# Moving every on-chip slot of a fused decoder layer to a 256-byte boundary

## The chip, the cores and the metric

The kernel runs on one core of a Trainium2 chip. The metric is the device time of one execution in microseconds (us); lower is better. SBUF is the on-chip memory; an address in it below is a byte address within one of its 128 partitions, the same in all of them. TensorE (PE) multiplies; VectorE (DVE), ScalarE (ACT) and GpSimd (POOL) do the rest; transfers are issued from SyncE's queue (SP).

## The reference

One layer on x of 1024 tokens by 1024 features, all in float32:

```
x = x + 0.5 * swiglu(rms_norm(x), w_gate, w_up, w_down)          # FF = 2816
h = rms_norm(x);  q,k,v,f | q,k,v | g_fox,g_sb = split(h @ w_in)
y_fox = softmax(q k^T/8 + cumulated log-forget-gates, causal) v   # 8 heads of 64
y_sb  = stick-breaking attention of the second q,k,v              # 8 heads of 64
x = x + (sigmoid(g_fox) * (y_fox @ w_branch_fox) + sigmoid(g_sb) * (y_sb @ w_branch_sb)) @ w_out
x = x + 0.5 * swiglu(rms_norm(x), ...)                            # second set of weights
x = x + sigmoid(rms_norm(x) @ w_ple_gate) * (p @ w_ple_proj)
```

## The kernel before

Every large product is done in the 32-bit reduced format (`float32r`) with each operand split into a high and a low part; three matmuls, high by high, high by low and low by high, stand for one. The split is an ACT copy and a subtraction (`split`, lines 103 and 104; `whigh` and `wlow`, lines 127 and 137). Most matmuls have a stationary operand of 128 by 128, which PE loads ahead of the matmul (an LDWEIGHTS, "PEld" in the profile), and a moving operand of 128 by 512 that is streamed through it. In the profile's `out<-a,b` of a matmul, a is the moving and b the stationary operand.

The work comes in this order, with the line of the matmul: the first FFN's gate and up products (lines 426 and 471, seven products in place of eight for each block of a two by two split), its down product (366), the projections of the attention stage (698, 706, 861), sixteen heads of attention (scores at 942 and 943, transposes at 994, values at 1016) woven with further projections, the branch products (706, 1223), the output product (366), the second FFN (426, 471, 366), and the gated embedding at the end (1490). Inside the two FFNs the order of all instructions is written out by hand; PE's own order is fixed by chained dependencies in the whole kernel. In an FFN the stationary operands of line 471 are split four products ahead (`prep`) into tiles whose tags rotate `("WL", "WL", "WL", "Q", "Q", "PT")`; the moving operands stay in tiles H, X and T.

All working tiles are slots of one pool, taken by tag in rotation:

```
BUFS = {"X": 2, "H": 4, "RAW": 2, "WH": 3, "WL": 3, "T": 4, "GF": 2, "RN": 2,
        "Q": 2, "KH": 2, "KL": 2, "Y": 2, "PT": 3}
```

A tag's slots are as large as its largest tile and stand one behind the other. X and H have 16,384 bytes a slot, the others 4096, except WH, WL and Y: these also hold a piece of `w_in` with 264 columns (256 of the values and 8 of the forget gates) as `[128, 4, 264]`, and so have 4224 bytes, 16.5 times 256. At address 0 stand 16,384 bytes of scratch for the descriptors of DMAs that software generates; the kernel issues none of these (its DMAs are all `nc.sync.dma_start` and one `nc.scalar.dma_start`). Behind them come four 32-byte constants, the kernel's own constants, small statistics, and from 19,328 (75.5 times 256) the slots.

That gives this remainder of the slots' start addresses divided by 256. All offsets within tiles at which the wide matmuls read are multiples of 256 bytes, so the remainder holds for the matmul's operand too. It is called the phase below.

| tag | before | after |
|---|---|---|
| X, PT, H, T, Q, GF, RN, RAW (all slots) | 128 | 0 |
| KH, KL (both slots) | 0 | 0 |
| WH | 128, 0, 128 | 0, 0, 0 |
| WL | 0, 128, 0 | 0, 0, 0 |
| Y | 128, 0 | 0, 0 |

The identity matrix for the transposes moves from phase 128 to 0 as well. Where the 264 columns are the moving operand, one row of them is 1056 bytes before (4 times 256 and 32) and 1088 after (4 times 256 and 64), so there the phase goes on by 32 or 64 from one block of 128 rows to the next.

Of the kernel before, what the change touches and what calls it, by code (L numbers as in the profile page):

```python
# [10 lines left out]
F32 = mybir.dt.float32  # L11
# [7 lines left out]
P = 128  # L19
# [11 lines left out]
BUFS = {"X": 2, "H": 4, "RAW": 2, "WH": 3, "WL": 3, "T": 4, "GF": 2, "RN": 2,  # L31
        "Q": 2, "KH": 2, "KL": 2, "Y": 2, "PT": 3}
# [4 lines left out]
def tile_hybrid_decoder_layer(  # L37
# [6 lines left out]
    nc = tc.nc  # L44
    cp = ctx.enter_context(tc.tile_pool(name="const", bufs=1))
    st = ctx.enter_context(tc.tile_pool(name="stats", bufs=4))
    sb = ctx.enter_context(tc.tile_pool(name="sb", bufs=2))
# [4 lines left out]
    def nm(s):  # L52
        uid[0] += 1
        return f"{s}_{uid[0]}"

    def slot(tag, shape, dt=F32):
        return sb.tile(shape, dt, tag=tag, bufs=BUFS[tag], name=nm(tag))

    def stat(shape, tag, bufs=4):
        return st.tile(shape, F32, tag=tag, bufs=bufs, name=nm(tag))  # L60
# [51 lines left out]
    def wraw_load(pieces, nk, n, tag="RAW"):  # L112
        raw = slot(tag, [P, nk, n])
        c = 0
        for src in pieces:
            w = src.shape[-1]
            nc.sync.dma_start(raw[:, :, c:c + w], src)
            c += w
        return raw
# [5 lines left out]
    def whigh(raw, nk, n, tag):  # L125
        hi = slot(tag, [P, nk, n], F32R)
        order("wh", nc.scalar.copy(hi[:], raw[:]))  # L127
        return hi

    def wlow(raw, hi, nk, n, tag, eng_lo=nc.gpsimd):  # L130
        lo = slot(tag, [P, nk, n], F32R)
        if nk == 1:
            parts = [(slice(None), slice(None), slice(i * n // 2, (i + 1) * n // 2)) for i in range(2)]
        else:
            parts = [(slice(None), slice(i * nk // 2, (i + 1) * nk // 2)) for i in range(2)]
        for part in parts:
            ins = eng_lo.tensor_sub(lo[part], raw[part], f(hi[part]))  # L137
            if eng_lo is nc.gpsimd:
                order("wl", ins)
        return lo  # L140

    def kp(w):
        return w.rearrange("(k p) n -> p k n", p=P)

    identf = cp.tile([P, P], F32, name="identf")
    make_identity(nc, identf[:])
    mask_fox = cp.tile([P, P], F32, name="mask_fox")
# [1399 lines left out]
```

## Time and profile before

| | |
|---|---|
| median of 3 runs | 2284.68 us (2284.53 to 2285.09) |
| span of the profiled execution | 2282.3 us |
| median less span (what lies around the span) | 2.4 us |
| PE busy in the span | 2260.2 us (99%) |
| DVE, ACT, POOL busy | 64%, 43%, 36% |
| granted TensorE clock | 1.00 in every stretch asked for |

The page gives the profiled execution's span and no time of its own beside it; the distance of 2.4 us between the runs' median and that span is carried over unchanged wherever a span is turned into a time. A matmul's duration in the profile contains its way through the array and overlaps the next matmul's; what a matmul costs in a row of them is the distance from its start to the next one's.

### The profile page before, as it was taken

Reading aid. Unit: us, or ns where it says so; the run is one execution under the profiler, and the core shown is the slowest. Engines: PE = TensorE matmul, PEld = TensorE weight load, DVE = VectorE, ACT = ScalarE, POOL = GpSimd, SP = SyncE. Lnnn points to the kernel's source line nnn. Section 1 sums busy time; section 2 is a strip of 40 time slices with the busy share of each in tenths; the row PEclk is TensorE's granted clock in tenths of the full one; section 3 lists DMA queues with packets and bytes.
Section 4 is the critical chain, followed back from the end, with each engine's and each line's share of the span. In section 5 each row is a group of like instructions: output and inputs, shape, how many; then the busy total and the mean of one; then the engine's idle time right before and its main releaser. Section 6 shows DMA issues by size and latency. Waiting matters only on the chain.

```text
span 2282.3 us, 30639 instructions
## 1 busy us (share of the span) xinstructions
PE 2260.2 (99%) x11462; PEld 1912.9 (84%) x11462; DVE 1459.6 (64%) x2199; ACT 977.7 (43%) x1741; POOL 828.1 (36%) x762
## 2 busy tenths in 40 slices
PE   8999999999999999999999999999999999999999
PEld 6888888888899999988988887888888888888887
DVE  8845555588863466666666675889655555778753
ACT  6333333333353555555555564245333333434431
POOL 2444444300033456554556654410544443200121
PEclk9999999999999999999999999999999999999999
DMA  4232323384333322132224245821423232656132
GB/s 139 102 116 84 125 83 125 137 315 158 115 120 118 99 86 74 48 89 70 52 56 116 61 150 173 298 109 59 139 84 125 83 125 79 259 193 218 63 102 84
DMA packets 187655, 275.49 MB, mean 121 GB/s; under 512 B 27113, under 2 KB 109417, under 8 KB 187506
## 3 DMA queue, kind: packets, MB, share of 16 engines
q1 hardware_dynamic: 187504, 273.53, 35.6%
q8 instruction: 90, 1.47, 0.3%
q14 instruction: 59, 0.48, 0.1%
q10 hardware_dynamic: 2, 0.00, 0.0%
HBM read 189.83 MB, written 75.27 MB: 116 GB/s over the span
## 4 chain that ended last, share of the span: by engine, by line
PE 94%; DVE 4%; ACT 1%; issue 1%; DMA 0%; DVEq 0%; ACTq 0%
PE ps L471 35%; PE ps L366 21%; PE ps L706 10%; PE ps L698 8%; PE ps L1490 4%; PE ps L1223 4%; PE ps L1016 3%; PE ps L994 2%; PE ps L426 1%; PE ps L943 1%; PE ps L942 1%; DVE RN L918 1%; PE ps L226 1%; PE ps L861 1%; DVE PT L997 0%
## 5 line engine op out<-in xcount | busy, mean ns | idle before, releaser
L366 PE MATMUL ps<-H,H 128*128 128x512 f32 x2184 | 497.8, 389 | 1.2 <-DVE X L374 1.2
L366 PEld LDWEIGHTS ps<-H,H 128*128 128x128 f32 x2184 | 409.4, 188 | 86.7 <-issue 2.0
L471 PE MATMUL ps<-H,WL 128*128 128x512 f32 x1008 | 244.3, 394 | 0.6 <-ACT WL L103 0.6
L471 PEld LDWEIGHTS ps<-H,WL 128*128 128x128 f32 x1008 | 189.7, 188 | 44.6 <-ACT WL L103 1.0
L706 PE MATMUL ps<-H,WH 128*128 128x512 f32 x768 | 210.5, 401 | 1.1 <-DVE PT L829 1.1
L706 PEld LDWEIGHTS ps<-H,WH 128*128 128x128 f32 x768 | 136.5, 188 | 24.4 <-DVE PT L829 1.6
L137 POOL TENSOR_TENSOR WL<-RAW,WH 128x512 fp32r<-128x512 f32 (+1 forms) x108 | 127.2, 1197 | 78.7 <-ACT WH L127 72.9
L137 POOL TENSOR_TENSOR WL<-Y,WH 128x512 fp32r<-128x512 f32 (+1 forms) x10 | 14.4, 1463 | 383.3 <-ACT WH L127 383.3
L997 DVE TENSOR_TENSOR PT<-ps,PT 128x512 fp32r<-128x512 f32 (+1 forms) x160 | 101.1, 633 | 76.0 <-ACT PT L996 74.9
L471 PE MATMUL ps<-H,Q 128*128 128x512 f32 x600 | 143.5, 390 | 0.0
L374 DVE SCALAR_TENSOR_TENSOR X<-ps,X 128x512 f32<-128x512 f32 x168 | 108.9, 685 | 50.9 <-PE ps L366 50.9
L698 PE MATMUL ps<-WH,H 128*128 128x256 f32 (+1 forms) x896 | 131.7, 286 | 1.9 <-DVE X L104 1.0
L471 PEld LDWEIGHTS ps<-H,Q 128*128 128x128 f32 x600 | 112.6, 188 | 23.9
L996 ACT CAST PT<-ps 128x512 fp32r<-128x512 f32 (+1 forms) x160 | 87.4, 548 | 95.6 <-PE ps L994 91.7
L471 PE MATMUL ps<-X,WL 128*128 128x512 f32 x504 | 123.5, 394 | 0.0
L698 PEld LDWEIGHTS ps<-WH,H 128*128 128x128 f32 x896 | 116.6, 189 | 3.7 <-DVE X L104 1.4
L471 PEld LDWEIGHTS ps<-X,WL 128*128 128x128 f32 x504 | 94.9, 188 | 21.8
L1016 PE MATMUL ps<-PT,X 128*128 128x256 f32 (+1 forms) x640 | 105.6, 283 | 5.9 <-DVE PT L997 5.8
L1016 PEld LDWEIGHTS ps<-PT,X 128*128 128x128 f32 x640 | 94.2, 189 | 18.6 <-DVE PT L997 9.3
L706 PE MATMUL ps<-H,WL 128*128 128x512 f32 x384 | 108.6, 399 | 0.0
L955 POOL TENSOR_TENSOR T<-T,l 128x128 f32<-128x128 f32 (+3 forms) x64 | 73.2, 1147 | 88.2 <-DVE l L954 85.8
L267 POOL TENSOR_TENSOR PT<-GF,RN 128x512 f32<-128x512 f32 x20 | 33.1, 1655 | 190.8 <-DVE GF L514 104.9
(400 smaller groups left out, 4737.2 us busy)
## 6 DMA issues: line engine op xcount, KB each, us to landing
hidden<-PT SPq DMA_DIRECT2D x40, 512.0 KB, 3.1
WH<-in_ffn_w_gate_dram SPq DMA_DIRECT2D x38, 512.0 KB, 5.3
Q<-hidden SPq DMA_DIRECT2D x24, 512.0 KB, 7.3
hidden<-RN SPq DMA_DIRECT2D x22, 512.0 KB, 2.6
RAW<-in_w_in_dram SPq DMA_DIRECT2D x22, 512.0 KB, 4.3
KH<-in_ffn_w_up_dram SPq DMA_DIRECT2D x20, 512.0 KB, 5.9
KL<-in_ffn_w_up_dram SPq DMA_DIRECT2D x20, 512.0 KB, 6.5
T<-in_ffn_w_down_dram SPq DMA_DIRECT2D x20, 512.0 KB, 4.2
```

The costliest lines, as they stand in the source:

```text
L137: ins = eng_lo.tensor_sub(lo[part], raw[part], f(hi[part]))
L366: pe(nc.tensor.matmul(groups[g][t][:], act[:, a, k, t * P:(t + 1) * P], wt[:, b, k, :], start=(fresh and n == 0), stop=(i in (6, 1, 4) and ...
L374: nc.vector.scalar_tensor_tensor(xs, groups[g][t][:], scale, xs, ALU.mult, ALU.add)
L471: pe(nc.tensor.matmul(ps[:], hl[:, a, k, :], rhs(m, b, k), start=(first and i == 0), stop=(final and i == 11), skip_group_check=True))
L698: pe(nc.tensor.matmul(ps[:, :n], hT[t // 4][a][:, k, (t % 4) * P:(t % 4 + 1) * P], w[k // 4][b][:, k % 4, :n], start=(i == 0), stop=(i == ...
L706: pe(nc.tensor.matmul(ps[:], w[a][:, k, :], hT[half][b][:, k, :], start=(i == 0), stop=(i == 23)))
L955: nc.gpsimd.tensor_mul(T[:, :n], T[:, :n], l[:].broadcast_to([P, n]))
L996: high = nc.scalar.copy(pt[:, 0, :width], ps[:, :width])
L997: low = nc.vector.tensor_sub(pt[:, 1, :width], ps[:, :width], f(pt[:, 0, :width]))
L1016: pe(nc.tensor.matmul(o, lh, r, start=(kpair == c and i == 0), stop=(kpair == 0 and i == 3)))
L1223: pe(nc.tensor.matmul(ps[:], w[a][:, k, :], yT[g][b][:, k, half * 512:half * 512 + 512], start=(i == 0), stop=(i == 11)))
L1490: pe(nc.tensor.matmul(ps, hT[t // 4][a][:, k, (t % 4) * P:(t % 4 + 1) * P], pl["w"][d, k // 2][b][:, k % 2, cs], start=(i == 0), stop=(i = ...
```

## The change

A slot whose last dimension is not a multiple of 16 elements is allocated with that dimension rounded up, and the tile handed out is the part without the padding. This touches the 264 columns alone: they become 272, and the slots of WH, WL and Y 4352 bytes, 17 times 256. An unused tile of 128 bytes is put ahead of the kernel's constants, so that the slots begin at 11,264, 44 times 256. The scratch is cut from 16,384 to 8192 bytes to make room. The instructions, their order on each engine, their shapes and the semaphores they wait for are the same; addresses differ, and the copies of the 264-column pieces go over four runs of 264 elements in place of one of 1056.

```diff
     def slot(tag, shape, dt=F32):
-        return sb.tile(shape, dt, tag=tag, bufs=BUFS[tag], name=nm(tag))
+        pad = -shape[-1] % 16
+        t = sb.tile([*shape[:-1], shape[-1] + pad], dt, tag=tag, bufs=BUFS[tag], name=nm(tag))
+        return t[:, :, :shape[-1]] if pad else t
...
+    cp.tile([P, 32], F32, name="lead")
     identf = cp.tile([P, P], F32, name="identf")
...
-    nc = _bacc.Bacc("TRN2", target_bir_lowering=False, num_devices=1)
+    nc = _bacc.Bacc("TRN2", target_bir_lowering=False, num_devices=1, dynamic_dma_scratch_size=8192)
```

## The prediction

> **What bounds the kernel now.** I read the page first: its busy shares and its chain.
>
> ```profile
> span 2282.3 us, 30639 instructions
> ...
> PE 2260.2 (99%) x11462; PEld 1912.9 (84%) x11462; DVE 1459.6 (64%) x2199; ACT 977.7 (43%) x1741; POOL 828.1 (36%) x762
> ...
> PE 94%; DVE 4%; ACT 1%; issue 1%; DMA 0%; DVEq 0%; ACTq 0%
> PE ps L471 35%; PE ps L366 21%; PE ps L706 10%; PE ps L698 8%; PE ps L1490 4%; PE ps L1223 4%; PE ps L1016 3%; PE ps L994 2%; PE ps L426 1%; PE ps L943 1%; PE ps L942 1%; DVE RN L918 1%; PE ps L226 1%; PE ps L861 1%; DVE PT L997 0%
> ```
>
> PE is busy all the time and 94% of the chain is its own; no DMA is on it. The change leaves every instruction and its order as it is, so it can act only through what an address does to an instruction's duration. What matters is the distance between matmuls of one size that read different slots. The groups by shape:
>
> ```profile
> L366 PE MATMUL ps<-H,H 128*128 128x512 f32 x2184 | 497.8, 389 | 1.2 <-DVE X L374 1.2
> ...
> L471 PE MATMUL ps<-H,WL 128*128 128x512 f32 x1008 | 244.3, 394 | 0.6 <-ACT WL L103 0.6
> ...
> L471 PE MATMUL ps<-H,Q 128*128 128x512 f32 x600 | 143.5, 390 | 0.0
> ```
>
> The same line, shape and moving tile takes 394 ns with its weights in WL and 390 with them in Q. WL has slots at phases 0, 128, 0 (the table of slots above), Q and H only at 128. Next the timeline of PE inside the first FFN, which keeps each product of twelve matmuls apart; columns are start, duration, and what ran:
>
> ```profile
> 310.43 2.89 PE L471 MATMUL ps<-X,PT 128*128 128x512 f32 x12
> 313.16 2.96 PE L471 MATMUL ps<-H,WL 128*128 128x512 f32 x12
> 315.95 2.92 PE L471 MATMUL ps<-T,WL 128*128 128x512 f32 x12
> 318.71 2.96 PE L471 MATMUL ps<-H,WL 128*128 128x512 f32 x12
> 321.50 2.91 PE L471 MATMUL ps<-H,Q 128*128 128x512 f32 x12
> 324.26 2.88 PE L471 MATMUL ps<-X,Q 128*128 128x512 f32 x12
> 326.98 2.89 PE L471 MATMUL ps<-H,PT 128*128 128x512 f32 x12
> ```
>
> By the layout, the WL tiles of 313.16, 315.95 and 318.71 lie at phases 0, 128 and 0; all else here is at 128. From start to start the products take 2.73 (PT), 2.79 (WL at 0), 2.76 (WL at 128), 2.79 (WL at 0), 2.76 (Q) and 2.72 us (the next Q). So it is not the tag: WL at 128 is quicker than WL at 0. A product at equal phases that follows one at unequal phases takes 2.76, and only the one after it 2.72, 226.7 ns a matmul; unequal phases cost 2.79, 232.5 ns. I read it as two streams, the moving operand and the weights being loaded for the next matmul, that settle into a smooth state when their phases are equal, need some matmuls to do so, and never do when they differ by 128.
>
> The doubt is whether equality counts or the value 128, since the trace has no matmul of this kind with both at 0. Line 861 has the roles turned round, the moving operand (WH, WL) at 0 and the stationary X at 128:
>
> ```profile
> 728.87 1.08 PE L861 MATMUL ps<-WH,X 128*128 128x512 f32 x4
> 729.80 0.63 PE L861 MATMUL ps<-WL,X 128*128 128x512 f32 x2
> 730.26 1.10 PE L861 MATMUL ps<-WH,X 128*128 128x512 f32 x4
> ...
> 733.05 1.10 PE L861 MATMUL ps<-WH,X 128*128 128x512 f32 x4
> ```
>
> Three rounds of 4 + 2 take 733.05 - 728.87 = 4.18 us, 232.2 ns a matmul: the same price whichever of the two is at 0. That is what a rule on the difference gives; a rule on each stream's own phase would need two causes that happen to cost the same. It is the main ground of the forecast.
>
> **The change part by part.** First the wide matmuls. The chain in order of time gives whole stretches (start, length, line, matmuls):
>
> ```profile
> 53.74 394.74 PE ps L471 x1716
> 448.49 125.16 PE ps L366 x552
> ...
> 1397.31 62.09 PE ps L1223 x270
> ...
> 1561.03 11.12 PE ps L426 x48
> 1572.15 398.51 PE ps L471 x1740
> ...
> 2187.66 5.54 PE ps L1490 x24
> ```
>
> The floor is line 366, all H by H at equal phases: 125.16 / 552 = 226.7 ns. After the change every operand of 512 columns is at phase 0, so I take this floor for all.
>
> - L471: 394.74 + 398.51 = 793.25 us for 3456; at the floor 3456 x 0.22674 = 783.6; 9.6 us go. The 72 others of the program's 3528 at the same 2.8 ns: 0.2. Together 9.8.
> - L426: 11.12 / 48 = 231.7, 5.0 ns over the floor, x192: 0.95.
> - L1223: 62.09 / 270 = 230.0, 3.2 ns, x384: 1.2.
> - L861: 232.2 - 226.7 = 5.5 ns for 48, and for the other 48, whose WH is at 128 and only WL at 0, something between nothing and that: 0.4.
> - L1490: 5.54 / 24 = 230.8, 4.1 ns, for the first half of the columns, 192 matmuls: 0.8. The second half has all its weights at 128 and stands at the floor already:
>
> ```profile
> 2251.10 1.07 PE L1490 MATMUL ps<-T,H 128*128 128x512 f32 x4
> ...
> 2256.54 1.07 PE L1490 MATMUL ps<-T,H 128*128 128x512 f32 x4
> ```
>
> 24 matmuls in 5.44 us, 226.7 each, with the moving operand changing among T, WH, WL, GF, RN and PT. Its WH slot and H differ by 256 modulo 512, so 256 is the modulus that counts; after the change WL and KH lie at 256 modulo 512 and others at 0, which this row says is harmless.
>
> For the attention stage the rows are less clean:
>
> ```profile
> L706 PE MATMUL ps<-H,WH 128*128 128x512 f32 x768 | 210.5, 401 | 1.1 <-DVE PT L829 1.1
> ...
> L698 PE MATMUL ps<-WH,H 128*128 128x256 f32 x768 | 114.7, 286 | 1.9 <-DVE X L104 1.0 <-ACT RN L763 0.7 <-DVE PT L829 0.2
> ...
> L698 PE MATMUL ps<-T,H 128*128 128x256 f32 x128 | 16.9, 284 | 0.0
> L942 PE MATMUL ps<-KH,Q 128*128 128x512 f32 x48 | 19.0, 395 | 0.0
> ```
>
> - Scores, KH and KL at 0 against Q at 128: 395 - 389 = 6 ns for the 96 with 512 columns (L942, L943): 0.6. The narrower ones at nothing.
> - L706: 401 against 389, but these run in short pieces between transposes, scores and values, and each break has to be settled anew. Ends: nothing, or 5.8 ns on all 1152 that the program has (WH and WL), 6.7 us. By the layout some 400 have unequal phases, 2.3 us if those alone settle; half of it, 1.2, because the pieces are short.
> - L698 (256 columns): WH, one slot of three at 0, takes 286, T at 128 takes 284, and that difference includes waits. From nothing to 2 ns x 768 = 1.5 us; I take nothing, as T's row is the nearer to what is left when the waits are taken off. The 264 columns, whose phases run through other remainders before and after, likewise.
>
> The sum is 9.8 + 0.95 + 1.2 + 0.4 + 0.8 + 0.6 + 1.2 = 14.95 us.
>
> What is late next? PE's feeders:
>
> ```profile
> PE ps L1016 <- DVE PT L997: 5.8, 10, 1.7
> ...
> PE ps L471 <- ACT WL L103: 0.6, 1, 0.6
> ```
> ```profile
> 30.00:430.00 400.00, 399.41 (x1743) 326.44 (x1742) 232.24 (x287) 144.92 (x257) 160.99 (x113) 1.00 0.29 99
> 760.00:1555.00 795.00, 783.60 (x4699) 691.23 (x4698) 533.82 (x1044) 416.74 (x849) 401.60 (x428) 1.00 0.34 105
> ```
>
> The second fence has, after the window, PE, PEld, DVE, ACT and POOL busy, the granted clock and the DMAs. In the FFN (first row) DVE works 232 of 400 us and the splits run four products, some 11 us, ahead; a PE quicker by 1.5% waits for nobody. In attention (second row) PE is idle 11.4 us of 795, mostly for DVE. There half of the gain of scores and L706, 0.9, may come back as such waits; for the other stages I take another 0.9. That leaves 13.2.
>
> **Transfers and the rest.** The same loads of the hidden values go to slots at 128 (GF) and at 0 (KH), with the median from issue to landing last:
>
> ```profile
> q1 hardware_dynamic: 187504, 273.53, 35.6%
> ...
> GF<-hidden SPq DMA_DIRECT2D x14, 512.0 KB, 9.0
> KH<-hidden SPq DMA_DIRECT2D x14, 512.0 KB, 9.2
> ```
>
> No gain from phase 0 shows, and no DMA is on the chain: nothing. [...] The padded copies of the 264 columns (four runs in place of one, two loads, on ACT and POOL) are issued in the last chunk of line 366, over a hundred matmuls ahead of their use in line 698, and hide behind these: nothing. Halving the scratch takes nothing from transfers that the hardware's queue carries: all issues are SP's and one is ACT's.
>
> **The rivals.** (a) The value 128 counts and not the equality: 0 is the bad phase for either stream, and two zeros cost as much as one. Then all 512-column matmuls come to 232.5: L366 5.8 x 2184 = +12.7, L471 3456 x 0.2325 - 793.25 = +10.3, L1223 2.5 x 384 = +1.0, L1490 5.8 x 168 + 1.7 x 192 = +1.3, L426 +0.2: 25.5 us, 2310. It decides from the first pass of line 366: 552 matmuls in 128.3 us in place of 125.16. For it: no pair at 0 and 0 exists here. Against it: line 861.
>
> (b) No change, 2284.7. [...] As a mechanism of this kernel: the spread between 2.72 and 2.79 us goes with what runs beside the product (its splits, its evictions) and stays when the addresses move. Against it: the WL product at 128 between two at 0.
>
> (c) The change does not reach its phase: 512 is the modulus. Then WL stays off in two of three slots as now, L471 keeps its 9.8 us, and only a little of the rest goes: some 1.5 us, 2283. Against it: the 5.44 us of line 1490.
>
> **How the numbers follow.** The profiled span of 2282.3 less 13.2 is 2269.1; with the 2.4 us that the median lies above the span, 2271.5. Its own range: 2267, where L706 gains its larger end's half and nothing is given back, to 2278, where L471 alone gains two thirds. Chances: forecast 0.77, (a) 0.14, (b) 0.05, (c) 0.04. The forecast's own range leaves a few hundredths outside, so for 8 in 10 the range reaches to 2284 and takes in (c). A measurement of this kernel can tell about 0.2%, 4.6 us. Faster by more: 0.77; within: 0.09, from (b) and (c); slower by more: 0.14, from (a).
>
> **What would show it.** In the profile after: L471's mean for WL falls to that for Q, 390; its two long pieces take 227 ns a matmul; L366 stays at 389 and 226.7. L861 and the first half of L1490 come to the floor, L698 stays. PE's busy time falls by about what the span does, and waits for DVE in attention grow by no more than 1 us. L366 above 226.7, or WL above Q, would make me wrong.

## Result and the profile after

The changed kernel takes 2273.84 us (median of 4 runs, 2273.46 to 2274.43), the kernel before 2284.89 us (2284.53 to 2285.30): 11.05 us less, a ratio of 0.9951 with a 95% interval of 0.9937 to 0.9965. Predicted were 2271.5 us, from 2267 to 2284.

The page of the changed kernel, where the line numbers are three higher than before:

```profile
span 2272.7 us, 30639 instructions
...
PE 2248.7 (99%) x11462; PEld 1912.6 (84%) x11462; DVE 1467.9 (65%) x2199; ACT 978.3 (43%) x1741; POOL 827.8 (36%) x762
...
PE 93%; DVE 4%; ACT 1%; issue 1%; DMA 0%; POOL 0%; DVEq 0%; ACTq 0%
```

PE lost 11.5 us of busy time with the same 11462 matmuls. ACT and POOL stayed within 0.6 us; DVE is busy 8.3 us longer, with the same 4% of the chain. The groups by shape (busy, mean ns of one, idle before):

```profile
L369 PE MATMUL ps<-H,H 128*128 128x512 f32 x2184 | 497.8, 389 | 1.2 <-DVE X L377 1.2
L474 PE MATMUL ps<-H,WL 128*128 128x512 f32 x1008 | 239.3, 389 | 0.8 <-ACT WL L105 0.8
L709 PE MATMUL ps<-H,WH 128*128 128x512 f32 x768 | 210.3, 401 | 1.1 <-DVE PT L832 1.1
L474 PE MATMUL ps<-H,Q 128*128 128x512 f32 x600 | 143.1, 389 | 0.0
...
L701 PE MATMUL ps<-WH,H 128*128 128x256 f32 x768 | 115.0, 287 | 1.9 <-DVE X L106 1.0 <-ACT RN L766 0.7 <-DVE PT L832 0.2
```

WL and Q are alike now, both at line 369's 389 ns, which did not move. Four consecutive products of the first FFN, of the same kinds as in the prediction's timeline (WL, WL, WL, Q):

```profile
310.87 2.88 PE L474 MATMUL ps<-H,WL 128*128 128x512 f32 x12
313.59 2.88 PE L474 MATMUL ps<-T,WL 128*128 128x512 f32 x12
316.31 2.88 PE L474 MATMUL ps<-H,WL 128*128 128x512 f32 x12
319.03 2.88 PE L474 MATMUL ps<-H,Q 128*128 128x512 f32 x12
```

Every start lies 2.72 us behind the one before, where the kernel before had 2.79, 2.76 and 2.79 for the three in WL and 2.76 for Q. The chain in order of time gives the stretches:

```profile
55.06 389.26 PE ps L474 x1716
444.31 125.13 PE ps L369 x552
...
750.63 5.44 PE ps L709 x24
...
1393.63 61.21 PE ps L1226 x270
...
1556.30 10.88 PE ps L429 x48
1567.18 394.40 PE ps L474 x1740
...
2178.56 5.47 PE ps L1493 x24
```

The two long pieces of the FFNs fell from 394.74 to 389.26 and from 398.51 to 394.40 us: 9.59 us of the 9.6 in the span. All other stages together came out at nothing, which was not forecast. Two losses stand against their gains. One belongs to this execution: the first matmuls wait for the first gain vector, and its transfer took 4.08 us where it had taken 2.72. That is 1.4 us; the other executions of the changed kernel have spans from 2271.7 to 2272.3, and in a later profile of the same kernel (the run after_again below) the wait is 3.9 us, against 5.2 here and 3.8 before. The other loss is in attention. Before, the last 24 matmuls of line 706 ahead of the heads start at 755.31:

```profile
755.31 5.45 PE ps L706 x24
```

From there to the long piece of line 1223 at 1397.31 were 642.00 us; after, from 750.63 to 1393.63, 643.00. The stage became 1.0 us longer, while PE's largest wait in it stayed (5.8 us before):

```profile
PE ps L1019 <- DVE PT L1000: 5.9, 10, 1.7
```

### The profile page after: what moved, and what is told of

Its sections match the earlier page's. It is cut to its first block, busy times and chain, and to the rows that moved or that the text cites. A ratio compares the mean times of both kernels' runs of the same rounds, so it can differ in the third digit from the quotient of the medians.

```text
span 2272.7 us, 30639 instructions
## 1 busy us (share of the span) xinstructions
PE 2248.7 (99%) x11462; PEld 1912.6 (84%) x11462; DVE 1467.9 (65%) x2199; ACT 978.3 (43%) x1741; POOL 827.8 (36%) x762
## 4 chain that ended last, share of the span: by engine, by line
PE 93%; DVE 4%; ACT 1%; issue 1%; DMA 0%; POOL 0%; DVEq 0%; ACTq 0%
PE ps L474 35%; PE ps L369 21%; PE ps L709 10%; PE ps L701 8%; PE ps L1493 4%; PE ps L1226 4%; PE ps L1019 3%; PE ps L997 2%; PE ps L946 1%; PE ps L945 1%; DVE RN L921 1%; PE ps L429 1%; PE ps L864 1%; PE ps L229 1%; DVE PT L1000 0%
## 5 line engine op out<-in xcount | busy, mean ns | idle before, releaser
L474 PE MATMUL ps<-H,WL 128*128 128x512 f32 x1008 | 239.3, 389 | 0.8 <-ACT WL L105 0.8
L709 PE MATMUL ps<-H,WH 128*128 128x512 f32 x768 | 210.3, 401 | 1.1 <-DVE PT L832 1.1
L709 PE MATMUL ps<-H,WL 128*128 128x512 f32 x384 | 108.3, 399 | 0.0
L921 DVE TENSOR_TENSOR_SCAN RN<-GF,RN 128x127 f32<-128x127 f32 (+2 forms) x96 | 99.1, 1032 | 2.7
```

Of the source, the lines that this page charges most:

```text
L474: pe(nc.tensor.matmul(ps[:], hl[:, a, k, :], rhs(m, b, k), start=(first and i == 0), stop=(final and i == 11), skip_group_check=True))
L709: pe(nc.tensor.matmul(ps[:], w[a][:, k, :], hT[half][b][:, k, :], start=(i == 0), stop=(i == 23)))
L921: order("dve", nc.vector.tensor_tensor_scan(*args))
```

## The experiments

**The pair of phases by itself.** A kernel with nothing but stretches of 48 matmuls, each with one moving and one stationary tile (8 elements are 32 bytes; the rest of the kernel is left out here):

```diff
...
+    for a in range(8):
+        for b in range(8):
+            n += 1
+            for i in range(48):
+                m = a * 8 + i % 4 * 512
+                s = b * 8 + i % 8 * P
+                nc.tensor.matmul(ps[n % 4][:], sta[b][:, s:s + P], mov[a][:, m:m + 512], start=(i == 0), stop=(i == 47))
...
```

> The disputed cost by itself: 64 stretches of 48 matmuls of 128x512 in float32r, each with one moving tile (ma to mh, its start at 0, 32, ... 224 modulo 256 bytes) and one stationary tile (sa to sh, the same eight starts); nothing of the layer is computed. Theory (the difference of the two phases modulo 256 counts): all stretches of one difference take the same; difference 0 takes 226.7 ns a matmul from start to start, among them ma with sa and me with se alike; difference 128 takes 232.5 in both directions. Rival (each stream's own phase counts, 128 good and 0 bad or the other way round): ma with sa and me with se differ by 5 ns or more. No theory says what differences of 32, 64 and 96 cost; if one of them is below 226.7 there is more to be had than this change takes.

PE's timeline, one row for each stretch:

```profile
69.37 11.32 PE L67 MATMUL psb<-ma,se 128*128 128x512 f32 x48
80.53 11.37 PE L67 MATMUL psc<-ma,sf 128*128 128x512 f32 x48
...
125.12 11.08 PE L67 MATMUL psc<-mb,sb 128*128 128x512 f32 x48
136.04 11.35 PE L67 MATMUL psd<-mb,sc 128*128 128x512 f32 x48
...
203.03 11.15 PE L67 MATMUL psb<-mc,sa 128*128 128x512 f32 x48
214.02 11.36 PE L67 MATMUL psc<-mc,sb 128*128 128x512 f32 x48
...
381.14 11.36 PE L67 MATMUL psb<-me,sa 128*128 128x512 f32 x48
392.34 11.36 PE L67 MATMUL psc<-me,sb 128*128 128x512 f32 x48
...
425.72 11.05 PE L67 MATMUL psb<-me,se 128*128 128x512 f32 x48
436.61 11.35 PE L67 MATMUL psc<-me,sf 128*128 128x512 f32 x48
```

From start to start, divided by 48: moving at 0 with stationary at 128 takes 232.5 ns (11.16 us), moving at 128 with stationary at 0 takes 233.3 (11.20); both at 128 take 226.9 (10.89) and both at 32 take 227.5 (10.92, with the step into the stretch). The difference counts: apart from the very first stretch, all those of one difference agree within 0.05 us. That first one, with both at 0, starts with PE's slow first matmuls (427 ns for the first ten) and its total is not used; from its twelfth matmul on it runs at 227, 227 and 226 ns like the others at difference 0, and the changed kernel has 2.72 us for 12. Moving 64 ahead of stationary is the second best, 229.0 (10.99). None of the eight differences goes below the one of 0 (the others take 229.0 to 234 ns), so steps of 32 bytes offered nothing more for these long runs of 512 columns.

**Everything at 128.** The changed kernel with one line less:

```diff
-    cp.tile([P, 32], F32, name="lead")
```

> The changed kernel without the 128 bytes ahead of the constants: padding kept, scratch halved, so all slots at 128 modulo 256 in place of 0. Theory (difference counts): the same gain, 2273.8 us within 1.5, L471's matmuls (line numbers shift) at 389 ns for WL and Q alike. Rival (0 is the good value by itself): back near 2284.9, or slower. Rival (scratch or the place of the constants brought the gain): something between.

```profile
L473 PE MATMUL ps<-H,WL 128*128 128x512 f32 x1008 | 239.4, 389 | 0.7 <-ACT WL L105 0.7
L473 PE MATMUL ps<-H,Q 128*128 128x512 f32 x600 | 143.2, 389 | 0.0
```

2273.29 us (2273.02 to 2273.34, 5 runs) against 2284.57 on the same chip, ratio 0.995 (0.9937 to 0.9964): the same gain with no slot at 0. The boundary of 256 bytes brings nothing by itself here.

**Without the padding.** The changed kernel with the old slot sizes:

```diff
-        pad = -shape[-1] % 16
-        t = sb.tile([*shape[:-1], shape[-1] + pad], dt, tag=tag, bufs=BUFS[tag], name=nm(tag))
-        return t[:, :, :shape[-1]] if pad else t
+        return sb.tile(shape, dt, tag=tag, bufs=BUFS[tag], name=nm(tag))
```

> The changed kernel without the padding: 128 bytes ahead of the constants and scratch halved, so that X, PT, H, T, Q, GF, RN, RAW are at 0, but WH at 0, 128, 0, KH and KL at 128, WL at 128, 0, 128, Y at 0, 128. Theory (difference counts): as many unequal pairs as in the kernel before, so no gain: 2284.9 us within 1.5, with WL 5 ns above Q again. Rival (the aligned start of the big tiles X, H, T or the smaller scratch brings a part of the gain, for transfers or other engines): 2276 to 2282.

```profile
L472 PE MATMUL ps<-H,WL 128*128 128x512 f32 x1008 | 244.2, 394 | 0.6 <-ACT WL L103 0.6
L472 PE MATMUL ps<-H,Q 128*128 128x512 f32 x600 | 143.5, 390 | 0.0
```

2284.60 us against 2284.57, ratio 1.000 (0.9991 to 1.0009). The big tiles lie at 0 here and the scratch is halved, and nothing is gained: the padding carries all of it, because it makes WH, WL, Y and what follows them equal to the rest. The lead and the smaller scratch bring nothing in these runs; the scratch makes room.

**The cost put back, larger.** One unused 128-byte tile ahead of WL and one behind Q:

```diff
+    gaps = []
...
+        gap = {"WL": "gapa", "GF": "gapb"}.pop(tag, None)
+        if gap and gap not in gaps:
+            gaps.append(gap)
+            sb.tile([P, 32], F32, tag=gap, bufs=1, name=gap)
```

> The changed kernel with one more unused tile of 128 bytes ahead of WL and one behind Q: WL, Y and Q at 128 modulo 256, everything else at 0. The suspected cost put back on purpose and made larger than it was: in line 471's products WL and Q are now both unequal to the moving H, X and T (2856 of 3528 matmuls in place of 1176). Theory (difference counts): 2856 x 6.1 ns = 17.4 us, and 2 us for the PT products that follow an unequal one, and about 1.5 us elsewhere: 21 us over the changed kernel, 2294 to 2296, slower than the kernel before by some 10 us. Rival (the gain came from transfers or other engines reaching aligned slots): at most 3 us over the changed kernel, since only two tags moved.

```profile
54.00 397.82 PE ps L480 x1716
...
1576.59 402.98 PE ps L480 x1740
```

2292.74 us (2292.41 to 2292.86) against 2284.53, ratio 1.0036 (1.0023 to 1.0048), 8.2 us slower than the kernel before. The two pieces are 17.14 us longer than in the changed kernel; 2856 x 6.1 ns had been put at 17.4. The 2 us for the PT products did not come, so the expected total was some 2 us too high; the rival's 3 us fail. A PT product at equal phases behind an unequal Q took 2.73 us here (312.69 to 315.42), not the 2.76 that the prediction had read off WL and Q: in this run such a product did not pay for the one ahead of it.

**Narrow and short.** Why did the attention stage gain nothing? Stretches of 256 columns with the stationary operand at 0, and stretches of 96 matmuls of 512 columns, cut into pieces by four transposes:

```diff
...
+    for a in range(8):
+        n += 1
+        for i in range(48):
+            m = a * 8 + i % 8 * 256
+            s = i % 8 * P
+            nc.tensor.matmul(ps[n % 4][:, 0:256], sta[0][:, s:s + P], mov[a][:, m:m + 256], start=(i == 0), stop=(i == 47))
+    for size in (2, 8, 24):
+        for a in (0, 2, 4):
+            n += 1
+            for r in range(96 // size):
+                for c in range(4):
+                    nc.tensor.transpose(tp[:, c * P:c * P + P], raw[:, c * P:c * P + P], identf[:])
+                for i in range(size):
...
```

> Why the attention stage gained nothing, by itself; nothing of the layer is computed. First eight stretches of 48 matmuls of 128x256 with the stationary tile sa (phase 0) and the moving tiles ma to mh (phases 0 to 224). Then nine stretches of 96 matmuls of 128x512, cut into pieces of 2, of 8 and of 24 by four transposes ahead of each piece, with the moving tiles ma, mc and me (differences 0, 64, 128) for each size. Theory (two streams settle after each break): with pieces of 24 difference 128 costs 3 to 6 ns a matmul more than difference 0, with pieces of 8 at most 2, with pieces of 2 nothing; with 256 columns difference 0 takes 120 ns and the others the same or up to 3 ns less. Rival (the price holds for each matmul, and attention's gain was lost to waits of other engines): 5 to 6 ns at every piece size, and at 256 columns too.

The stretches of 256 columns:

```profile
42.24 5.92 PE L71 MATMUL psb<-ma,sa 128*128 128x256 f32 x48
48.00 5.82 PE L71 MATMUL psc<-mb,sa 128*128 128x256 f32 x48
53.66 5.82 PE L71 MATMUL psd<-mc,sa 128*128 128x256 f32 x48
...
65.06 5.86 PE L71 MATMUL psb<-me,sa 128*128 128x256 f32 x48
70.76 5.86 PE L71 MATMUL psc<-mf,sa 128*128 128x256 f32 x48
```

Difference 0 takes 5.76 / 48 = 120.0 ns, difference 32 takes 117.9, and 128 takes 118.8. At 256 columns equal phases are the slowest of the eight: difference 96 takes 119.8 ns, the others 117.7 to 118.8. Each difference was run in one stretch only. The pieces of 8, by the first transpose of each stretch of 96 and of the next (differences 0, 64, 128):

```profile
217.96 0.60 PE L77 MATMUL turn<-identf,raw 128*128 128x128 f32 x4
...
245.47 0.60 PE L77 MATMUL turn<-identf,raw 128*128 128x128 f32 x4
...
273.00 0.60 PE L77 MATMUL turn<-identf,raw 128*128 128x128 f32 x4
...
300.57 0.60 PE L77 MATMUL turn<-identf,raw 128*128 128x128 f32 x4
```

That is 27.51, 27.53 and 27.57 us: 0.6 ns a matmul between 0 and 128. With pieces of 24 (first at difference 0, then at 128):

```profile
300.92 5.73 PE L81 MATMUL psd<-ma,sa 128*128 128x512 f32 x24
306.50 0.60 PE L77 MATMUL turn<-identf,raw 128*128 128x128 f32 x4
...
348.43 5.82 PE L81 MATMUL psb<-me,sa 128*128 128x512 f32 x24
354.09 0.60 PE L77 MATMUL turn<-identf,raw 128*128 128x128 f32 x4
```

That is 5.58 against 5.66 us, 3.3 ns a matmul. The pieces of 2 missed: nothing was expected, and their stretches of 96 took 43.21 us at difference 0 and 43.46 at 128, 2.5 ns a matmul.

The starts of the single matmuls in this trace show the settling itself. In the second piece of 24 at difference 0 they follow one another by 314, 235, 234, 235, 225, 230, 236, 229, 232 and 231 ns, and from the eleventh on by 226 or 227, up to the last but one. At difference 128 the matmuls behind the first stay between 228 and 241 to the end of the piece. Over the pieces of 24, the second to seventh matmuls take 231.8 ns on average at difference 0 and 232.9 at 128; the ninth to the last but one take 227.2 and 232.2. So the gain of equal phases started some ten matmuls behind a break here. A piece of 8 ends before that, at 232.4 against 232.8 ns for its second to seventh. In pieces of 2, difference 128 costs 3 ns from the first matmul to the second (317 against 314) and 3 ns from the second to the next transpose (234 against 231).

**The changed kernel again, and a version that follows from this.** The first is the changed kernel as it is. The second places the moving weights of the 256-column projections 64 bytes into their slots, and the stationary values of line 1016 likewise; where a piece has 264 columns, its rows lie 1056 bytes apart again:

```diff
+    def wtile(tag, nk, n, off):
+        if off:
+            return slot(tag, [P, 1088], F32R)[:, 16:16 + nk * n].rearrange("p (k n) -> p k n", k=nk)
+        return slot(tag, [P, nk, n], F32R)
...
-                cell["v"] = slot("X", [P, NT, 4, P], F32R)
+                cell["v"] = slot("X", [P, 4160], F32R)[:, 16:4112].rearrange("p (t h d) -> p t h d", t=NT, h=4)
```

> The changed kernel once more, to stand beside the next one on the same chip: 2273.5 us within 1, and in its profile the stretch from the first score matmul to the branch products again 0.5 to 1.2 us longer than in the kernel before, if that loss belongs to the equal phases and not to one profiled execution.

> The changed kernel with the moving operands of the 256-column projections (line 698 in the kernel before) placed 64 bytes into their slots, and the stationary values of line 1016 likewise, so that matmuls of 256 columns have a difference of 64 or 192 and those of 512 keep 0. Theory (the isolated stretches: 256 columns take 120.0 ns at difference 0 and 117.8 at 64 and 192, but only in long runs): line 698 has 1344 such matmuls, half of them in long runs, so 1.5 to 3 us less, line 1016 up to 0.5: 2270.5 to 2272.5, and the attention stage falls by 1 us or more. Rival (attention is bound by its chain through DVE and ACT): within 0.5 us of the changed kernel.

2273.10 us (2273.06 to 2273.15) and 2270.20 us (2269.63 to 2270.36), 5 runs each on one chip, against 2284.40 for the kernel before: ratios 0.9951 (0.9938 to 0.9963) and 0.9938 (0.9924 to 0.9951). The second is 2.9 us faster than the changed kernel and the fastest of all. The ratios' intervals overlap, but no run of the one reaches a run of the other. The first score matmul in the kernel before, and then the first score matmul and the long piece of the branch products without and with the 64 bytes:

```profile
760.60 0.22 PE L942 MATMUL ps<-KH,Q 128*128 128x128 f32 x1
```
```profile
754.58 0.22 PE L945 MATMUL ps<-KH,Q 128*128 128x128 f32 x1
```
```profile
1392.29 61.23 PE ps L1226 x270
```
```profile
754.59 0.22 PE L950 MATMUL ps<-KH,Q 128*128 128x128 f32 x1
```
```profile
1389.53 61.23 PE ps L1231 x270
```

The stage between takes 637.71 and 634.94 us, 2.8 less, and nearly the whole gain. The loss of the changed kernel is confirmed as well: the same stretch had 636.71 us in the kernel before (760.60 to 1397.31), 1.0 less than 637.71. The other profiles agree: 637.73 in the changed kernel's first profile (755.90 to 1393.63) and 637.60 with everything at 128 (754.76 to 1392.36), but 636.94 without the padding (760.64 to 1397.58). The largest group of the projections shows where the 64 bytes act (line 706 of this kernel is line 698 of the kernel before):

```profile
L706 PE MATMUL ps<-WH,H 128*128 128x256 f32 x768 | 113.5, 284 | 1.9 <-DVE X L106 1.0 <-ACT RN L771 0.7 <-DVE PT L837 0.2
```

It has 284 ns in place of 287, with DVE's wait the same. The rival, that attention is bound by DVE and ACT, falls.

## Why the prediction was right

**Equality, not the value.** The step that carried the forecast, read from the roles turned round in line 861, held: the grid gives 232.5 and 233.3 ns for the two directions, and a kernel with everything at 128 gains as much as one with everything at 0. Rival (a) is refuted by line 369, 125.13 us for 552. Rival (b) falls with the 17.14 us put back, and (c) with WL at 389 ns in slots at 256 and 0 modulo 512.

**The sizes by line.** L471: forecast 9.6 in the two pieces, measured 9.59. L426: 11.12 to 10.88 for 48 in the second FFN, as forecast; in the first FFN nothing came, for from one and the same matmul of line 426 to the long piece of line 471 it took 35.62 us before (18.12 to 53.74) and 35.58 after (19.48 to 55.06). L1223: 0.87 forecast and 62.09 to 61.21, 0.88. L861: 11.16 and 11.03 to 10.91 and 10.88, 0.40 as forecast. L1490: 5.54 to 5.47 for a piece, 0.07 where the floor had promised 0.10. All operands at the floor was right for the runs that are long.

**The terms that were mis-sized** are mostly in the attention stage. L706 was put at 1.2 us between 0 and 6.7; its two groups went from 210.5 to 210.3 and from 108.6 to 108.3 us, 0.5 together. The doubt written beside it, that each break has to be settled anew, was the right one, and half was too much: in the stage's trace this line comes almost only in pieces of 4 to 6 matmuls and never in more than 11, and the gain started only some ten matmuls behind a break (226 or 227 ns from the eleventh on in a piece of 24). The scores of line 942 came from 395 to the row below, half of the 6 ns; those of line 943 only from 393 to 392.

```profile
L945 PE MATMUL ps<-KH,Q 128*128 128x512 f32 x48 | 18.8, 392 | 0.0
```

L698 was taken at nothing with a bound of a gain, and that was the wrong sign: 286 became 287 ns, and the isolated stretches of 256 columns are slowest at equal phases (120.0 ns against 117.7 to 119.8). Line 1016, which the forecast does not price, lost as much (before, then after):

```profile
L1016 PE MATMUL ps<-PT,X 128*128 128x256 f32 x512 | 103.3, 290 | 5.5 <-DVE PT L997 5.5
```
```profile
L1019 PE MATMUL ps<-PT,X 128*128 128x256 f32 x512 | 103.6, 291 | 5.6 <-DVE PT L1000 5.6
```

Its own operands PT and X are at equal phases in both kernels, so its loss does not follow from its own pair. That it comes from the neighbours whose weights are loaded beside it is possible, but not shown.

**Give-back.** 0.9 us was put aside for new waits on DVE in attention. The waits did not grow (5.8 to 5.9 us); the stage did lose 1.0 us, and the 256-column matmuls of lines 698 and 1016 are where it shows. The version with 64 bytes took that loss back and more. The other 0.9 us, for the other stages, was used up, though not by waits on DVE that the forecast had in mind: with attention at a loss of 1.0, the 11.05 us leave 12.05 for the rest, against terms of 13.15, and L426 in the first FFN is the largest part of the gap that is known. So the 13.2 us of the forecast come down to 11.05 mainly because short and narrow matmuls were counted as gains or as nothing: attention was to bring 0.9 and lost 1.0. That the two margins of 0.9 together came near what was missing is luck.

**From span to time.** The 2.4 us carried over is not a constant of this kernel: every later execution for which both are on record has its time 1.7 to 1.8 us above its span (2274.43 and 2272.7 for the profiled one). By that the same sum would have given 2270.8 us. The span fell by 9.6 and the medians by 11.05; the difference is about the 1.4 us of the first transfer, which are in the one profiled execution only.

## What to carry to other kernels

Where TensorE is the bound, list for each matmul the start address modulo 256 of its moving operand and of the weights loaded beside it, before anything else is moved: one odd tile size (264 columns) had shifted five tags, and a padding of 32 bytes a row got 0.5% back here. Equal remainders are what counted for long runs of 512 columns (226.9 ns against 229.0 to 234), not any boundary (ratio 0.995 with everything at 128, 0.9951 at 0); behind a break the gain took some ten matmuls to set in (226 or 227 ns from the eleventh of 24 on). Measure the narrower shapes by themselves: what was best for 512 columns was worst for 256 (120.0 ns against 117.7 to 119.8).

## What the hardware showed that was not expected

In the isolated stretches the cost depends on the difference of the two addresses modulo 256, and with a sign: moving 64 ahead of stationary takes 229.0 ns, stationary 64 ahead of moving 233.4, and the others 232 to 234, except 226.9 for equal ones. The stretches of busy time from 69 us on (PE, PEld, DVE, ACT, POOL, granted clock, DMA share, GB/s) show nobody else at work:

```profile
69.00:700.00 631.00, 631.00 (x2721) 510.83 (x2720) 0.00 (x0) 0.00 (x0) 0.00 (x0) 1.00 0.00 1
```

So the difference, 232.5 against 226.9 ns, arises while TensorE works alone, and it follows the addresses of TensorE's two operands. The runs do not show what in that work brings it about.

At 256 columns the order is turned round, 120.0 ns at difference 0 and 117.9 at 32. Why it turns was not found.
